# FFN up projection: from two pairs of chunks by Winograd's form to three by Strassen's, spread over three blocks, one sum of weights per pair by accumulating transfers

## The chip, the cores and the metric

The kernel runs on one core of a Trainium2 chip. TensorE (PE) multiplies, VectorE (DVE), ScalarE (ACT) and GpSimd (POOL) do the rest, each engine working through its own instructions in order. Transfers are issued from SyncE's queue (SP), a few from ACT's, and, in the changed kernel, some from POOL's. The metric is the device time of the kernel in microseconds (us); the time before is the median of three runs.

## The reference

Two layers of a decoder trunk. Each layer has an FFN (a), a mixer of three branches, an FFN (b) and a small embedding step. The change is in the FFN alone, which runs four times.

```python
SEQ, D_MODEL, D_FF, DEPTH = 256, 1024, 2816, 2
def swiglu(x, w1, w3, w2):
    return (jax.nn.silu(x @ w1) * (x @ w3)) @ w2
...
h = h + 0.5 * swiglu(rms_norm(h, g_ffn1[i]), w1_a[i], w3_a[i], w2_a[i])
...
h = h + 0.5 * swiglu(rms_norm(h, g_ffn2[i]), w1_b[i], w3_b[i], w2_b[i])
```

## The kernel before

*Numbers.* Every fp32 operand of a matmul is split into a high part (ACT casts it to fp32r: whi, xhi, fhi) and a low part (DVE subtracts: wlo, xlo, flo). mm3 (L102 to L104) makes one product of three matmuls: high by high, high x by low w, low x by high w. In the rows of PE the first name behind the arrow is the weight tile, the second the activations.

*Tiles.* The 2816 columns of an FFN are 11 chunks (c = 0 to 10) of 256 columns of w1 and the same of w3, side by side: 512 columns. The 256 tokens are two blocks (tb). A chunk's weights come as four units of 128x1024 fp32 (512 KB, two rows of k by 512 columns); load() fetches a unit into raw on SP's queue and splits it (L86, L87). A unit is used by 12 matmuls of 128x512, a plain chunk by 48. up(c) runs a whole chunk; up_unit(c, i) runs unit i of it (called unit (c, i) or P(c, i) below), so that other work can stand between the units. gated() makes silu(w1 part) x (w3 part) out of PSUM into pr (L236 on ACT, L238 on DVE). turn(c) (T) transposes a chunk's two pr tiles on PE (L250) into one PSUM bank and splits the result into fhi and flo. down_unit(c, j) (D) fetches a unit of w2 and adds 12 matmuls into the four acc banks. PSUM holds two mm banks, two tr banks and these four. There are 7 slots each for whi and wlo, 4 for raw, 10 for wr (wtile), which holds weights that are summed before they are split, and 4 for t512, which holds products.

*Pairs.* Two neighbouring chunks by two halves of k are a 2x2 block matrix. A fast algorithm makes its product with the 2x2 of tokens by halves of k in 7 products of 12 matmuls each instead of 8. x_forms() makes the sums of x's quarters that it needs: DVE adds high and low parts, rescales the second token block (L297), for which the row scale is spread over the partitions by one matmul with ones (L274) and a copy to rb on ACT, and then forms and splits five quarters (q). winograd(c, fx) fetches the pair's 8 tiles and returns make (the split of a weight form), form (a sum of weights on DVE, L320) and the generator of the products (tr banks; L345 and L352 combine them).

*Order.* Each engine's instructions stand largely in the order in which the program is written; the framework moves some by priority. In an FFN, chunks 0, 1 and 2 come first and plain, x_forms() is called behind chunk 1; then block() runs twice, each time one pair (7, 8 and 9, 10) with eight units of two plain chunks (3, 4 and 5, 6), transposes and down units between them by hand-written tables; at the end come D5, T6, T10, D6, T9, and the last four down units with the update of h.

## Time and profile before

| what | before |
|---|---|
| median of three runs | 1333.03 us (1332.51 to 1333.06) |
| the profiled execution | 1332.86 us |
| its span in the profile | 1331.1 us |
| the fourth FFN | 1112.66 to 1297.00 us |

The span runs from the first to the last instruction in the trace; the execution's own time is 1.8 us longer. In rows of the profile, L12 is line 12 of the kernel, a name left of the arrow is written, names right of it are read, and buffer numbers are left out, so wr stands for every wr tile. A bracket behind a row of the timeline tells how long the engine was idle before it, and what released it.

### The profile page before, as it was taken

What the parts mean: (1) busy time and instruction counts of PE and PEld (TensorE: products, weight loads), DVE (VectorE), ACT (ScalarE), POOL (GpSimd) and SP (SyncE); (2) the same over time, 40 slices, a digit from 0 to 9 for tenths busy, and PEclk for the clock granted to TensorE, in tenths of its full rate; (3) what the DMA queues carried; (4) which work ended last, traced back from release to release, by engine and by line L of the source; (5) the groups of instructions that cost most, each with busy time, mean ns of one, the idle gap of its engine ahead of it and who ended that gap; (6) DMA issues with size and microseconds to landing.
All of it is one profiled execution on the core that took longest, in us unless ns stands there. A gap on an engine that the chain in (4) does not pass through costs nothing.

```text
span 1331.1 us, 17969 instructions
## 1 busy us (share of the span) xinstructions
PE 1312.2 (99%) x6624; PEld 1097.5 (82%) x6624; DVE 994.0 (75%) x1414; ACT 802.8 (60%) x1205; POOL 50.2 (4%) x109
## 2 busy tenths in 40 slices
PE   9999999999999999999999999999999999999997
PEld 7788879978888888887888888898888788888876
DVE  7998755666768789975789986566676677999755
ACT  6665546665775655654756665466667835655645
POOL 1000000001100000000100000000010000000001
PEclk9999999999999999999999999999999999999999
DMA  8774537534455567455566646373444465583542
GB/s 296 274 269 127 187 103 228 171 123 132 147 169 175 161 227 276 122 164 182 163 239 196 217 128 210 103 224 127 159 142 143 144 204 167 206 299 102 180 145 80
DMA packets 67769, 236.63 MB, mean 178 GB/s; under 512 B 8160, under 2 KB 8800, under 8 KB 67680
## 3 DMA queue, kind: packets, MB, share of 16 engines
q1 hardware_dynamic: 67104, 234.39, 54.0%
q8 instruction: 52, 0.85, 0.3%
q10 hardware_dynamic: 576, 1.08, 0.2%
q14 instruction: 37, 0.30, 0.1%
HBM read 234.40 MB, written 1.05 MB: 177 GB/s over the span
## 4 chain that ended last, share of the span: by engine, by line
PE 94%; ACT 2%; DVE 2%; DMA 1%; issue 1%; POOL 0%; SPq 0%; POOLq 0%; ACTq 0%; DVEq 0%
PE mm L102 17%; PE mm L104 17%; PE mm L103 17%; PE acc L102 8%; PE acc L103 8%; PE acc L104 8%; PE tr L104 4%; PE tr L102 4%; PE tr L103 4%; PE tr L250 1%; PE tr L150 1%; ACT whi L86 1%; PE tr L716 1%; DVE wlo L87 1%; DMA h<-in_x 1%
## 5 line engine op out<-in xcount | busy, mean ns | idle before, releaser
L87 DVE TENSOR_TENSOR wlo<-raw,whi 128x1024 fp32r<-128x1024 f32 (+1 forms) x378 | 450.1, 1201 | 137.3 <-ACT whi L86 135.1
L86 ACT CAST whi<-raw 128x1024 fp32r<-128x1024 f32 (+1 forms) x378 | 387.3, 1035 | 198.2 <-PE mm L104 77.5
L102 PE MATMUL mm<-whi,xhi 128*128 128x512 f32 (+1 forms) x760 | 296.0, 393 | 0.0
L103 PE MATMUL mm<-wlo,xhi 128*128 128x512 f32 (+1 forms) x760 | 295.1, 389 | 0.3 <-DVE wlo L87 0.3
L104 PE MATMUL mm<-whi,xlo 128*128 128x512 f32 (+1 forms) x760 | 295.2, 389 | 0.0
L102 PEld LDWEIGHTS mm<-whi,xhi 128*128 128x128 f32 x760 | 143.0, 188 | 30.0 <-DVE sqk L516 0.7
L104 PEld LDWEIGHTS mm<-whi,xlo 128*128 128x128 f32 x760 | 142.8, 188 | 29.7 <-DVE xlo L136 0.7
L103 PEld LDWEIGHTS mm<-wlo,xhi 128*128 128x128 f32 x760 | 142.9, 188 | 28.9 <-DVE wlo L87 0.8
L135 ACT CAST whi<-wr 128x1024 fp32r<-128x1024 f32 (+1 forms) x120 | 121.6, 1023 | 66.9 <-PE acc L104 38.9
L136 DVE TENSOR_TENSOR wlo<-wr,whi 128x1024 fp32r<-128x1024 f32 (+1 forms) x120 | 140.6, 1185 | 24.8 <-ACT whi L135 23.6
L102 PE MATMUL acc<-whi,fhi 128*128 128x512 f32 x352 | 132.0, 393 | 7.7 <-ACT fhi L135 7.7
L103 PE MATMUL acc<-wlo,fhi 128*128 128x512 f32 x352 | 137.9, 392 | 0.4 <-DVE wlo L87 0.4
L104 PE MATMUL acc<-whi,flo 128*128 128x512 f32 x352 | 134.6, 390 | 0.0
L102 PEld LDWEIGHTS acc<-whi,fhi 128*128 128x128 f32 x352 | 65.7, 188 | 23.2 <-ACT fhi L135 9.6
L103 PEld LDWEIGHTS acc<-wlo,fhi 128*128 128x128 f32 x352 | 66.1, 188 | 15.2 <-DVE wlo L87 1.8
L104 PEld LDWEIGHTS acc<-whi,flo 128*128 128x128 f32 x352 | 66.1, 188 | 13.6
L320 DVE TENSOR_TENSOR wr<-wr,wr 128x1024 f32<-128x1024 f32 x64 | 76.3, 1217 | 0.0
L102 PE MATMUL mm<-xhi,whi 128*128 128x256 f32 x256 | 73.8, 288 | 0.0
L104 PE MATMUL mm<-xhi,wlo 128*128 128x256 f32 x256 | 72.5, 283 | 0.0
L103 PE MATMUL mm<-xlo,whi 128*128 128x256 f32 x256 | 72.4, 283 | 0.0
L102 PE MATMUL tr<-whi,q 128*128 128x512 f32 x160 | 63.7, 398 | 0.0
L104 PE MATMUL tr<-whi,q 128*128 128x512 f32 x160 | 62.6, 391 | 0.0
(248 smaller groups left out, 1960.8 us busy)
## 6 DMA issues: line engine op xcount, KB each, us to landing
raw<-in_w13b SPq DMA_DIRECT2D x56, 512.0 KB, 3.7
raw<-in_w13a SPq DMA_DIRECT2D x52, 512.0 KB, 4.2
raw<-in_wg SPq DMA_DIRECT2D x48, 512.0 KB, 3.7
raw<-in_w2a SPq DMA_DIRECT2D x44, 512.0 KB, 4.4
raw<-in_w2b SPq DMA_DIRECT2D x44, 512.0 KB, 4.3
wr<-in_w13a SPq DMA_DIRECT2D x32, 512.0 KB, 6.7
raw<-in_wqk SPq DMA_DIRECT2D x32, 512.0 KB, 4.1
wr<-in_w13b SPq DMA_DIRECT2D x32, 512.0 KB, 6.2
```

Of the source, the lines that this page charges most:

```text
L86: A.copy(hi[:, c], raw[:, c])
L87: V.tensor_tensor(out=lo[:, c], in0=raw[:, c], in1=hi[:, c].bitcast(F32), op=ALU.subtract)
L102: PE.matmul(o, lhs[0], rhs[0], start=first, stop=False, **more)
L103: PE.matmul(o, lhs[0], rhs[1], start=False, stop=False, **more)
L104: PE.matmul(o, lhs[1], rhs[0], start=False, stop=last, **more)
L135: A.copy(hi, t)
L136: V.tensor_tensor(out=lo, in0=t, in1=hi.bitcast(F32), op=ALU.subtract)
L150: PE.transpose(t[:, j * P : (j + 1) * P], h[tb][:, k * P : (k + 1) * P], ident)
L250: PE.transpose(t[:, j * S + tb * P : j * S + (tb + 1) * P], prs[c, tb][:, j * P : (j + 1) * P], ident)
L320: V.tensor_tensor(out=out, in0=a, in1=b, op=ALU.subtract)
L716: PE.transpose(t[:, j * P : (j + 1) * P], e[:, j * P : (j + 1) * P], ident)
```

## The change

Three pairs instead of two, (5, 6), (7, 8) and (9, 10), with Strassen's seven products in the order 1, 2, 5, 3, 6, 7, 4. A pair's quarters are x, y, w, z; the sums of weights are x+=w, then x+=z, w+=z and y+=x, and w+=z is made by two transfers on POOL's queue, which read z again from memory and add it to the tile. Five chunks are left plain: 0 and 1 first, 2, 3 and 4 spread over three blocks. What a block runs is now one list: S is a step of the pair (split the weights of the next product, make a sum, run one product), P a unit of a plain chunk, D a down unit, T a transpose. wr has 12 slots and t512 has 5. The lines behind the FFN are numbered 26 higher.

```diff
--- before.py
+++ after.py
...
         with tc.tile_pool(name=nm("fp"), bufs=3) as fp:
             def wtile():
-                return fp.tile([P, U], F32, tag="wr", name=nm("wr"), bufs=10)
+                return fp.tile([P, U], F32, tag="wr", name=nm("wr"), bufs=12)
             def t512(name):
-                return fp.tile([P, 512], F32, tag="t512", name=nm(name), bufs=4)
+                return fp.tile([P, 512], F32, tag="t512", name=nm(name), bufs=5)
             if first:
                 un0 = start(wtile)
...
                     if tb:
                         V.tensor_tensor(out=v4(t), in0=v4(t), in1=rb[:, None, :].to_broadcast([P, 4, P]), op=ALU.mult)
                 f = {1: [x[:, 0, 0:4, :] for x in (xhi, xlo)], 2: [x[:, 0, 4:8, :] for x in (xhi, xlo)]}
-                V.tensor_tensor(out=s1, in0=a10, in1=a11, op=ALU.add)
+                sub(s1, a10, a11)
                 f[5] = quarter(s1)
                 sub(s1, s1, a00)
                 f[6] = quarter(s1)
                 sub(a10, a00, a10)
                 f[7] = quarter(a10)
-                sub(a01, a01, s1)
+                V.tensor_tensor(out=a01, in0=a01, in1=s1, op=ALU.add)
                 f[3] = quarter(a01)
                 f[4] = quarter(a11)
                 return f
-            def winograd(c, fx):
-                ws, t2s, fw = [], [], {}
-                for u in range(2):
-                    ws.append({(kh, nh): wtile() for kh in range(2) for nh in range(2)})
-                for kh, nh in ((0, 0), (1, 0), (0, 1), (1, 1)):
+            ORDER = (1, 2, 5, 3, 6, 7, 4)
+            def pair(c, bank):
+                t = {q: [wtile() for _ in range(2)] for q in "xywz"}
+                fw = {}
+                quarters = {"x": (0, 0), "y": (1, 0), "w": (0, 1), "z": (1, 1)}
+                def at(q, u):
+                    kh, nh = quarters[q]
+                    return w13[li, c + nh, 2 * kh + u]
+                def fetch(q):
                     for u in range(2):
-                        nc.sync.dma_start(ws[u][kh, nh], w13[li, c + nh, 2 * kh + u])
-                def sub(out, a, b):
-                    V.tensor_tensor(out=out, in0=a, in1=b, op=ALU.subtract)
+                        nc.sync.dma_start(t[q][u], at(q, u))
+                def add(q, other):
+                    for u in range(2):
+                        V.tensor_tensor(out=t[q][u], in0=t[q][u], in1=t[other][u], op=ALU.add)
+                def plus(q, other):
+                    for u in range(2):
+                        nc.gpsimd.dma_start(t[q][u], at(other, u), accum_op=ALU.add)
                 def form(i):
-                    for u, w in enumerate(ws):
-                        if i == 1:
-                            sub(w[0, 0], w[0, 1], w[0, 0])
-                        elif i == 2:
-                            t2s.append(wtile())
-                            sub(t2s[u], w[1, 1], w[0, 0])
-                        elif i == 3:
-                            sub(w[0, 1], w[1, 1], w[0, 1])
-                        else:
-                            sub(w[1, 0], w[1, 0], t2s[u])
+                    if i == 1:
+                        add("x", "w")
+                    elif i == 2:
+                        add("x", "z")
+                    elif i == 3:
+                        plus("w", "z")
+                    else:
+                        add("y", "x")
                 def make(i):
-                    at = {1: (0, 0), 2: (1, 0), 7: (0, 1), 5: (0, 0), 3: (1, 1), 4: (1, 0)}
-                    fw[i] = [split_w(t2s[u] if i == 6 else w[at[i]]) for u, w in enumerate(ws)]
+                    fw[i] = [split_w(w) for w in t[{1: "x", 2: "y", 5: "x", 3: "z", 6: "x", 7: "w", 4: "y"}[i]]]
                 def product(o, i, start=False):
                     for kt in range(4):
                         m = [y[:, (kt % 2) * 512 : (kt % 2) * 512 + 512] for y in fw[i][kt // 2]]
                         mm3(o, [y[:, kt, :] for y in fx[i]], m, start and kt == 0, kt == 3, skip_group_check=True)
-                def add(out, a, b):
-                    V.tensor_tensor(out=out, in0=a, in1=b, op=ALU.add)
+                def sum_(out, a, b, op=ALU.add):
+                    V.tensor_tensor(out=out, in0=a, in1=b, op=op)
                 def products():
-                    o = bank_tr()
+                    o = bank()
                     product(o, 1, True)
                     m1 = t512("m1")
                     A.copy(m1, o)
...
                     product(o, 2)
                     gated(c, 0, o, r[0])
                     yield
-                    o = bank_tr()
+                    o = bank()
+                    product(o, 5, True)
+                    c5 = t512("c5")
+                    A.copy(c5, o)
+                    yield
+                    product(o, 3)
+                    v = t512("v")
+                    A.copy(v, o)
+                    yield
+                    o = bank()
                     product(o, 6, True)
                     u2 = t512("u2")
-                    add(u2, o, m1)
+                    sum_(u2, o, m1)
+                    sum_(v, v, u2, ALU.subtract)
+                    gated(c + 1, 0, v, r[0])
                     yield
                     product(o, 7)
-                    add(m1, o, m1)
+                    sum_(m1, o, m1)
+                    sum_(c5, c5, m1, ALU.subtract)
+                    gated(c + 1, 1, c5, r[0])
                     yield
-                    o = bank_tr()
-                    product(o, 5, True)
-                    c22 = t512("c22")
-                    add(c22, o, m1)
-                    gated(c + 1, 1, c22, r[0])
-                    yield
-                    product(o, 3)
-                    add(u2, o, u2)
-                    gated(c + 1, 0, u2, r[0])
-                    yield
-                    o = bank_tr()
+                    o = bank()
                     product(o, 4, True)
-                    add(m1, o, m1)
+                    sum_(m1, o, m1)
                     gated(c, 1, m1, r[0])
                     yield
-                return make, form, products()
-            def block(wg, plain, turns, downs, then=None):
-                make, form, ps = wg
+                return make, fetch, form, products()
+            def block(now, plan, then=None):
+                make, _, form, ps = now
                 following = None
                 os = []
-                for k in range(8):
-                    if k < 6:
-                        make((2, 6, 7, 5, 3, 4)[k])
-                    if k < 3:
-                        form(k + 2)
-                    if k == 6 and then is not None:
-                        following = winograd(then, fx)
-                    if k == 7 and then is not None:
-                        following[0](1)
-                        following[1](1)
-                    if k < 7:
+                k = 0
+                for kind, *arg in plan:
+                    if kind == "S":
+                        if k < 6:
+                            make(ORDER[k + 1])
+                        if k < 4:
+                            form((1, 2, 3, 4)[k])
+                        if then is not None:
+                            if k == 2:
+                                following = pair(*then)
+                                following[1]("x")
+                            elif k == 3:
+                                following[1]("y")
+                            elif k == 4:
+                                following[1]("w")
+                            elif k == 5:
+                                following[1]("z")
+                            elif k == 6:
+                                following[0](1)
                         next(ps)
-                    if k % 4 == 0:
-                        os = []
-                    up_unit(plain[k // 4], k % 4, os)
-                    if k in downs:
-                        down_unit(*downs[k])
-                    for t in turns.get(k, ()):
-                        turn(t)
+                        k += 1
+                    elif kind == "P":
+                        if arg[1] == 0:
+                            os = []
+                        up_unit(*arg, os)
+                    elif kind == "D":
+                        down_unit(*arg)
+                    else:
+                        turn(*arg)
                 return following
-            for c in range(3):
+            for c in range(2):
                 if first and c == 1:
                     un = []
...
                 if c == 1:
                     acc.extend(bank_acc() for _ in range(4))
                     fx = x_forms()
-                    wg = winograd(7, fx)
+                    wg = pair(5, bank_tr)
+                    for q in "xywz":
+                        wg[1](q)
                 if c >= 1:
                     turn(c - 1)
             wg[0](1)
-            wg[1](1)
-            for j in range(2):
-                down_unit(0, j)
             if first:
                 later()
-            wg = block(
-                wg, (3, 4), {0: [2], 4: [3]},
-                {0: (1, 0), 1: (1, 1), 2: (2, 0), 3: (2, 1), 5: (3, 0), 6: (3, 1)}, 9,
-            )
+            wg = block(wg, [
+                ("S",), ("P", 2, 0), ("D", 0, 0), ("S",), ("P", 2, 1), ("S",), ("D", 0, 1), ("P", 2, 2), ("S",),
+                ("T", 1), ("P", 2, 3), ("S",), ("D", 1, 0), ("S",), ("D", 1, 1), ("S",), ("T", 2),
+            ], (7, bank_tr))
+            wg = block(wg, [
+                ("S",), ("P", 3, 0), ("D", 2, 0), ("S",), ("T", 6), ("P", 3, 1), ("D", 2, 1), ("S",),
+                ("P", 3, 2), ("T", 5), ("D", 6, 0), ("S",), ("P", 3, 3), ("D", 6, 1), ("S",), ("D", 5, 0),
+                ("S",), ("D", 5, 1), ("T", 3), ("S",),
+            ], (9, bank_tr))
             if aside is not None:
                 aside()
-            block(
-                wg, (5, 6), {0: [4], 1: [7], 2: [8], 5: [5]},
-                {1: (4, 0), 2: (4, 1), 3: (7, 0), 4: (7, 1), 5: (8, 0), 6: (8, 1)},
-            )
-            for j in range(2):
-                down_unit(5, j)
-            turn(6)
-            turn(10)
-            for j in range(2):
-                down_unit(6, j)
-            turn(9)
+            wg = block(wg, [
+                ("S",), ("P", 4, 0), ("D", 3, 0), ("S",), ("T", 8), ("P", 4, 1), ("D", 3, 1), ("S",), ("T", 7),
+                ("P", 4, 2), ("D", 8, 0), ("S",), ("P", 4, 3), ("D", 8, 1), ("S",), ("D", 7, 0), ("S",),
+                ("D", 7, 1), ("T", 4), ("S",), ("T", 10),
+            ])
+            block((None, None, None, iter(())), [
+                ("D", 4, 0), ("T", 9), ("D", 4, 1),
+            ])
```

What this moves, at three places of the fourth FFN. First DVE, at the start of block 1. Before:

```order
L87 TENSOR_TENSOR wlo_10835<-raw_10833,whi_10834 128x1024
L136 TENSOR_TENSOR pT_11444<-xg_11445,pT_11443 128x512
L238 SCALAR_TENSOR_TENSOR pr_10719<-mm_10692,r_10503,act_10717 128x256
L87 TENSOR_TENSOR wlo_10841<-raw_10839,whi_10840 128x1024
L238 SCALAR_TENSOR_TENSOR pr_10748<-mm_10721,r_10558,act_10746 128x256
L297 TENSOR_TENSOR wr_10763<-wr_10763,rb_10761 128x512 x2
L136 TENSOR_TENSOR flo_10813<-tr_10814,fhi_10812 128x512
L299 TENSOR_TENSOR wr_10765<-wr_10763 128x512
L284 TENSOR_TENSOR wr_10763<-wr_10764,wr_10763 128x512
```

Before, DVE splits chunk 2's last units (L87, wlo from raw) and gates chunk 1 (L238) ahead of the forms of x, which begin with L297. After, from the forms on (they stand directly behind chunk 1's two rows of L238):

```order
L297 TENSOR_TENSOR wr_10865<-wr_10865,rb_10863 128x512 x2
L136 TENSOR_TENSOR flo_10915<-tr_10916,fhi_10914 128x512
L284 TENSOR_TENSOR wr_10867<-wr_10865 128x512
L284 TENSOR_TENSOR wr_10865<-wr_10866,wr_10865 128x512
L136 TENSOR_TENSOR q_10876<-wr_10867,q_10875 128x512
L284 TENSOR_TENSOR wr_10867<-wr_10867,wr_10866 128x512
L305 TENSOR_TENSOR wr_10866<-wr_10866,wr_10867 128x512
L136 TENSOR_TENSOR q_10881<-wr_10867,q_10880 128x512
L136 TENSOR_TENSOR q_10886<-wr_10865,q_10885 128x512
L136 TENSOR_TENSOR q_10891<-wr_10866,q_10890 128x512
L136 TENSOR_TENSOR q_10895<-wr_10865,q_10894 128x512
L136 TENSOR_TENSOR wlo_10924<-wr_10898,whi_10923 128x1024
```

Eleven rows with twelve operations make the forms (and one flo of chunk 0), and the first weights that DVE splits behind them are the first pair's: wlo from wr, 128x1024.

PE at the same place, before:

```order
L104 MATMUL mm_10721<-whi_10687,xlo 128x512
L274 MATMUL tr_10759<-xg_10757,ones 128x128
L250 MATMUL tr_10814<-ident,pr_10637 128x128 x2
L250 MATMUL tr_10814<-ident,pr_10666 128x128 x2
L102 MATMUL mm_10845<-whi_10822,xhi 128x512
L103 MATMUL mm_10845<-wlo_10823,xhi 128x512
```

and after:

```order
L104 MATMUL mm_10823<-whi_10789,xlo 128x512
L274 MATMUL tr_10861<-xg_10859,ones 128x128
L250 MATMUL tr_10916<-ident,pr_10739 128x128 x2
L250 MATMUL tr_10916<-ident,pr_10768 128x128 x2
L102 MATMUL tr_10941<-whi_10923,xhi 128x512
L103 MATMUL tr_10941<-wlo_10924,xhi 128x512
```

mm and whi from chunk 2 follow the transposes (L250) before, product 1 of the pair (tr and whi from wr) after.

Last, PE's tail. Before:

```order
L104 MATMUL acc_10753<-whi_11945,flo_11838 128x512
L250 MATMUL tr_11964<-ident,pr_11920 128x128 x2
L250 MATMUL tr_11964<-ident,pr_11924 128x128 x2
L250 MATMUL tr_11973<-ident,pr_11799 128x128 x2
L250 MATMUL tr_11973<-ident,pr_11736 128x128 x2
L102 MATMUL acc_10750<-whi_11981,fhi_11962 128x512
L103 MATMUL acc_10750<-wlo_11982,fhi_11962 128x512
```

and after:

```order
L102 MATMUL acc_10852<-whi_12117,fhi_12080 128x512
L103 MATMUL acc_10852<-wlo_12118,fhi_12080 128x512
L250 MATMUL tr_12109<-ident,pr_12016 128x128 x2
L250 MATMUL tr_12109<-ident,pr_12060 128x128 x2
L104 MATMUL acc_10852<-whi_12117,flo_12081 128x512
L102 MATMUL acc_10853<-whi_12117,fhi_12080 128x512
L103 MATMUL acc_10853<-wlo_12118,fhi_12080 128x512
L104 MATMUL acc_10853<-whi_12117,flo_12081 128x512
```

Before, the transposes of chunks 6 and 10 stand side by side, and the next acc matmul reads the fhi that comes of the first of them. After, chunk 10's transposes stand among the matmuls of D(4,0), which read another fhi.

## The prediction

> **What bounds the kernel now.** First the page's busy rows and its chain of waits, then the stalls of TensorE (PE), then one FFN by itself, since the change touches nothing else.

> ```profile
> PE 1312.2 (99%) x6624; PEld 1097.5 (82%) x6624; DVE 994.0 (75%) x1414; ACT 802.8 (60%) x1205; POOL 50.2 (4%) x109
> ...
> PE 94%; ACT 2%; DVE 2%; DMA 1%; issue 1%; POOL 0%; SPq 0%; POOLq 0%; ACTq 0%; DVEq 0%
> ...
> PE acc L102 <- ACT fhi L135: 7.7, 8, 1.2
> ```

> PE is busy 99% of the span and carries 94% of the chain: a matmul taken away is worth its full pitch, and a PE stall costs its full length. The third row (waits of PE: us, times, the longest) is the largest stall inside the FFNs. Now windows over all engines: the fourth FFN, a piece of it with dense VectorE (DVE) work, and a piece of plain matmuls. The columns are length, then busy time of PE, PEld, DVE, ACT and POOL, then the granted clock, the DMA share and GB/s.

> ```profile
> 1112.66:1297.00 184.34, 182.41 (x831) 150.25 (x829) 147.64 (x168) 103.90 (x131) 2.02 (x6) 1.00 0.56 187
> 1142.46:1177.00 34.54, 34.54 (x156) 28.32 (x156) 34.53 (x34) 22.03 (x25) 0.00 (x0) 1.00 0.60 202
> 1192.69:1209.01 16.32, 16.32 (x73) 13.51 (x72) 16.20 (x18) 8.88 (x10) 0.00 (x0) 1.00 0.41 122
> ```

> An FFN takes 184.34 us with PE idle for 1.9 of them. In the third row 72 matmuls of 128x512 take 16.32 us, so the pitch is 0.227 us at a granted clock of 1.00. In the second row DVE is busy 34.53 of 34.54 us and PE loses nothing: DVE can be full without holding PE up.

> **The change part by part.** The sum is made against the profiled execution (span 1331.1, its own time 1332.86 us; the median of the runs is 1333.03, so the forecast carries over within 0.2).

> *Matmuls.* A third pair replaces two plain chunks: 7 products of 12 matmuls, where two plain chunks have 96. That is 12 fewer per FFN, 12 x 0.227 = **-2.72 us**, wholly on PE's path.

> *The tail.* Before, two transposed chunks (L250) stand back to back and the next matmul needs their copies at once:

> ```profile
> 1273.52 1.04 PE L250 MATMUL tr<-ident,pr 128*128 128x128 f32 x8
> 1275.30 0.50 PE L102 MATMUL acc<-whi,fhi 128*128 128x512 f32 x1 [0.74 <-ACT fhi L135]
> ...
> 1280.90 0.60 PE L250 MATMUL tr<-ident,pr 128*128 128x128 f32 x4
> 1282.68 0.50 PE L102 MATMUL acc<-whi,fhi 128*128 128x512 f32 x1 [1.18 <-ACT fhi L135]
> ```

> Transposes cost about 0.09 us each (8 begin and end within 1.04), so from 1273.52 to 1275.30 about 1.08 us pass for nothing, and from 1280.90 to 1282.68 about 1.4; I take 2.3 for both, with the overlap of the last transpose off. The new tail puts chunk 10's transposes among the matmuls of D(4,0) and chunk 9's ahead of D(4,1), which needs neither; 12 matmuls, 2.72 us, cover 1.18. **-2.3 us** per FFN. Nothing else is late there: the weights of the last units are requested early in both.

> *The start of block 1.* This term decides. The forms of x (x_forms) wait for one matmul (L274) behind chunk 1. Their DVE chain, and behind it the split of the first pair's weights, run like this before, in the fourth FFN:

> ```profile
> 1133.42 0.60 PE L250 MATMUL tr<-ident,pr 128*128 128x128 f32 x4
> 1133.77 0.47 PE L102 MATMUL mm<-whi,xhi 128*128 128x512 f32 x1
> ...
> 1134.30 1.29 DVE L297 TENSOR_TENSOR wr<-wr,rb 128x512 f32<-128x512 f32 x2
> 1135.50 0.68 DVE L136 TENSOR_TENSOR flo<-tr,fhi 128x512 fp32r<-128x512 f32 x1
> 1136.11 0.68 DVE L299 TENSOR_TENSOR wr<-wr 128x512 f32<-128x512 f32 x1
> 1136.82 0.69 DVE L284 TENSOR_TENSOR wr<-wr,wr 128x512 f32<-128x512 f32 x1
> 1137.48 0.69 DVE L136 TENSOR_TENSOR q<-wr,q 128x512 fp32r<-128x512 f32 x1
> 1138.20 1.42 DVE L284 TENSOR_TENSOR wr<-wr,wr 128x512 f32<-128x512 f32 x2
> 1139.58 2.50 DVE L136 TENSOR_TENSOR q<-wr,q 128x512 fp32r<-128x512 f32 x4
> 1142.00 0.48 DVE L238 SCALAR_TENSOR_TENSOR pr<-mm,r,act 128x256 f32<-128x256 f32 x1
> 1142.46 2.36 DVE L136 TENSOR_TENSOR wlo<-wr,whi 128x1024 fp32r<-128x1024 f32 x2
> ...
> 1141.02 0.47 ACT L236 ACTIVATE act<-mm,r 128x256 f32<-128x256 f32 x1
> 1141.38 1.99 ACT L135 CAST whi<-wr 128x1024 fp32r<-128x1024 f32 x2
> ```

> Before, PE steps at 1133.77 straight into plain chunk 2 (48 matmuls, 48 x 0.227 = 10.9 us), whose weights were split ahead of the chain; the chain ran beside it and cost nothing. In the new order of instructions chunk 2 is spread over block 1, and behind the transposes of chunk 0 PE has product 1. Its weights are split on DVE and on ScalarE (ACT) behind the whole chain, in all four FFNs. The cover is gone. The chain keeps its 12 operations, since L305 only turns a difference into a sum. ACT no longer has the activation of 1141.02, so its cast of the first tile starts there and ends at 1141.02 + 1.04 = 1142.06; DVE's subtraction follows, 1.22, until 1143.28. PE has one matmul (0.23) to do between, with whi alone. The hole is 1143.28 - 1133.77 - 0.23 = **+9.3 us** per FFN. Bounds: 8.3 us, if the subtraction overlapped the cast wholly, and 10.9, the cover that goes.

> *Behind the hole.* Two things, of which the later counts. On DVE the first split is followed by three more of weights, two sums and then the low half of unit (2,0), at 1.14 us each (2.36 - 1.22): 6.8 us. PE has 26 matmuls until it needs it, 5.9 us: a wait of 0.9. The other is the clock:

> ```profile
> 1323.15 0.28 PE L104 MATMUL mm<-whi,xlo 128*128 128x256 f32 x1
> ...
> 1326.60:1327.00 0.40, 0.00 (x0) 1.00 0.00 0
> 1327.00:1327.40 0.40, 0.00 (x0) 0.56 0.00 0
> ...
> 0.97 4.63 PE L992 MATMUL tr<-ones 128*128 128x128 f32 x20 [0.97 <-POOL mhalf L72]
> 5.47 0.99 PE L102 MATMUL mm<-whi,xhi 128*128 128x512 f32 x2
> 6.30 0.64 PE L103 MATMUL mm<-wlo,xhi 128*128 128x512 f32 x2
> ```

> At the end of the program PE's last matmul ends at 1323.43, and the granted clock falls to half at about 1327.0: 3.6 us of idleness. At its start the matmuls of 5.47 are 0.41 us apart and those from 6.30 on 0.24: some 5.3 us of work pass before PE is at speed. The hole holds 8.3 us without a matmul, so the clock would fall, and 5 us at about half rate lose 2.5. Bounds: 0.9 (the clock doesn't fall: the wait alone) and 2.7. I take **+2.5**, the only rows that show a cold PE; PE is then late enough for the weights.

> [...]

> *Work beside PE.* Per FFN DVE gets 8 more operations of 1024 columns (the splits of six weight tiles, two sums; 8 x 1.14 = 9.1 us) and five more of 512 on products (0.69 each, 3.4 us): about 160 of 185 us, still less dense than the window above. ACT gets six casts (1.0 each) and seven copies: 104 + 11 us. Both hide beside PE; bounds nothing, and one 1.14 us where a split comes last. Between blocks product 1 waits for a PSUM bank that a sum of 0.69 us reads: between 0 and 0.7, I take **+0.3**.

> *Accumulating transfers* (one sum per pair, two of 512 KB on POOL's queue). Before has none. The nearest rows are the plain ones, issue to landing:

> ```profile
> raw<-in_w13b SPq DMA_DIRECT2D x56, 512.0 KB, 3.7
> ...
> wr<-in_w13b SPq DMA_DIRECT2D x32, 512.0 KB, 6.2
> ```

> In block 1 they may start after x+=w, and DVE reaches the split of their result 16 operations later, 15 of about 1.14 and one of 0.48: at least 17.5 us; in blocks 2 and 3 later still. At the price of the plain ones to the same tiles, one behind the other, both have landed after 2 x 6.2 = 12.4; if each took twice that because it reads two operands, after 24.8. I take 12.4, the nearest row, and so **nothing** on the path; bounds 0 and 24.8 - 17.5 = 7.3 per FFN. What they spare DVE is in the list above already.

> *SP's queue.* In the first FFN alone, two weight tiles of chunk 1's down projection now stand behind fetches of the next pair, which wait for tiles to come free. Cost: between 0 and one landing, 3.7; I take 0.5, since only the excess over their lead counts.

> Sum: -2.72 - 2.3 + 9.3 + 2.5 + 0.3 = +7.1 per FFN, x4 = 28.3, and 0.5: 1332.86 + 28.8 = 1361.7, say **1361**.

> **The rivals.** *A, faster: the split runs ahead of the forms.* If the hardware's order let the first pair's weights be split before L274, product 1 would start at 1133.77, and only -2.72 - 2.3 with 0.3 remained: -4.7 x 4, 1314. The point from which it decides: hole and its wake together under 4.7 us per FFN. For it: the tiles are loaded early and nothing in the data ties them to the forms. Against it: engines work their rows in order, and the split's rows stand behind the chain on both; the pair's tiles can't pass it.

> *B, far slower: the accumulating transfers are late.* At 24.8 us each pair, block 1 loses 7.3 and DVE's queue stands still behind the split; blocks 2 and 3, with about 24 us by the same count, lose about 1 each: +9.3 x 4 = 37 on top, about 1399. For it: every transfer now reads its target too. Against it: 17.5 us are nearly three of the slower landings. [...]

> *C, milder: the hole without a colder clock.* Then the wake is 0.9 and all is 1332.86 + 4 x 5.5 + 0.5 = 1355.

> *D, no change:* that the matmuls aren't saved is excluded by the order (48 fewer); for no change the hole and its wake would have to come to about 4.7 us.

> **How the numbers follow.** The forecast 0.62 (1361), C 0.20 (1355), B 0.08 (1399), A 0.07 (1314), D 0.03. The low end is C with the hole at 8.3 instead of 9.3: 1351, and 0.5 less on SP's queue, rounded to 1350. The high end is the forecast with the hole 1.6 longer (10.9, x4 = 6.4), 0.4 more for the bank and 1.14 for a late split, each x4: 1373, and 3.7 for SP: 1377. About 0.15 to 0.2 lies outside. A measurement of this kernel tells about 0.2% from no change: faster 0.07, same 0.03, slower 0.90.

> **What would show it.** In the changed kernel, four PE waits of 8 to 9 us at product 1 of block 1, released by ACT's whi or DVE's wlo; half a clock in a window just behind them; no more wait for fhi in the tail; the FFN otherwise shorter by the 5 us of the first two terms. A wait of DVE or ACT for POOL's queue ahead of product 7 would be rival B. If product 1 starts right behind L250, I am wrong.

## The result and the profile after

| what | before | after |
|---|---|---|
| median of three runs | 1333.03 us | 1355.51 us (1354.1 to 1359.27) |
| the profiled execution, its span | 1332.86, 1331.1 | 1355.51, 1353.7 |
| end of FFN 1, 2, 3, 4 (last update of h) | 195.0, 639.2, 852.7, 1297.0 | 198.7, 649.5, 868.8, 1319.3 |
| what FFN 1, and 2 to 4 with the mixers ahead of them, got longer | | 3.7, 6.6, 5.8, 6.3 |

The ratio is 1.0171 with a 95% interval of 1.0148 to 1.0194: slower, by 22.5 us, where 28 were forecast.

The changed kernel's page, its busy rows and its chain by engine:

```profile
PE 1308.6 (97%) x6576; PEld 1093.2 (81%) x6576; DVE 1042.0 (77%) x1466; ACT 837.2 (62%) x1257; POOL 69.5 (5%) x133
...
PE 91%; DVE 5%; issue 1%; ACT 1%; DMA 1%; SPq 0%; POOLq 0%; POOL 0%; ACTq 0%
```

The 48 matmuls are gone (6576 where there were 6624), but PE's share of the span fell from 99 to 97%, and DVE stands on the chain with 5% instead of 2. PE's largest waits in the changed kernel (us, times, the longest) say for whom:

```profile
PE tr L102 <- ACT whi L135: 32.3, 4, 8.1
PE tr L103 <- DVE wlo L136: 1.9, 4, 0.5
```

Four waits of 8.1 us, one in each FFN, and the tail's waits for fhi (7.7 us before) no longer stand in the list. The place is the one forecast. Here is the fourth FFN of the changed kernel, first PE, then DVE, then ACT, from the timeline:

```profile
1149.39 0.39 PE L274 MATMUL tr<-xg,ones 128*128 128x128 f32 x2
1149.61 0.60 PE L250 MATMUL tr<-ident,pr 128*128 128x128 f32 x4
1158.29 0.80 PE L102 MATMUL tr<-whi,xhi 128*128 128x512 f32 x1 [8.08 <-ACT whi L135]
1159.55 0.80 PE L103 MATMUL tr<-wlo,xhi 128*128 128x512 f32 x1 [0.46 <-DVE wlo L136]
...
1150.50 1.28 DVE L297 TENSOR_TENSOR wr<-wr,rb 128x512 f32<-128x512 f32 x2
...
1155.77 2.50 DVE L136 TENSOR_TENSOR q<-wr,q 128x512 fp32r<-128x512 f32 x4
1158.27 4.63 DVE L136 TENSOR_TENSOR wlo<-wr,whi 128x1024 fp32r<-128x1024 f32 x4
...
1155.12 2.18 ACT L135 CAST q<-wr 128x512 fp32r<-128x512 f32 x4 [1.49 <-DVE wr L284]
1157.20 3.88 ACT L135 CAST whi<-wr 128x1024 fp32r<-128x1024 f32 x4
```

PE is ready at about 1150.0 and steps into product 1 at 1158.29, when ACT has cast the first tile; the second matmul waits once more, for DVE. DVE works without a gap from 1150.50 on, and the split of the first pair's weights is its first row behind the forms: the bracket of PE names ACT's cast, but what PE truly waits for is the chain of forms ahead of it. The granted clock there (length, PE's busy time, clock, DMA share, GB/s; PE alone):

```profile
1150.00:1152.00 2.00, 0.21 (x2) 1.00 0.95 387
1152.00:1153.00 1.00, 0.00 (x0) 0.85 0.09 37
1153.00:1158.00 5.00, 0.00 (x0) 0.50 0.10 18
1158.00:1162.00 4.00, 3.24 (x7) 0.50 0.28 109
1162.00:1163.00 1.00, 1.00 (x4) 0.53 0.00 0
1163.00:1164.00 1.00, 1.00 (x6) 1.00 0.00 0
```

The clock falls to half within the hole, and PE works at half rate from 1158.3 to 1162.9: its matmuls start 0.43 us apart, against 0.23 behind that. Last the accumulating transfers, issue to landing:

```profile
wr<-in_w13a POOLq DMA_DIRECT2D x12, 512.0 KB, 5.6
wr<-in_w13b POOLq DMA_DIRECT2D x12, 512.0 KB, 5.6
```

With a median of 5.6 us they are no slower than the plain ones were (6.2 and 6.7 to the same tiles before). The two of a first block, which are issued 0.9 to 1.1 us apart, land one behind the other, though: the pair is there 9.5 to 11.2 us after the first was issued.

### The profile page after: what moved, and what is told of

It reads as the page before. It is cut to its first block, busy times and chain, and to the rows that moved or that the text cites. A ratio compares the mean times of both kernels' runs of the same rounds, so it can differ in the third digit from the quotient of the medians.

```text
span 1353.7 us, 18041 instructions
## 1 busy us (share of the span) xinstructions
PE 1308.6 (97%) x6576; PEld 1093.2 (81%) x6576; DVE 1042.0 (77%) x1466; ACT 837.2 (62%) x1257; POOL 69.5 (5%) x133
## 3 DMA queue, kind: packets, MB, share of 16 engines
q10 hardware_dynamic: 576, 1.08, 0.2%
## 4 chain that ended last, share of the span: by engine, by line
PE 91%; DVE 5%; issue 1%; ACT 1%; DMA 1%; SPq 0%; POOLq 0%; POOL 0%; ACTq 0%
PE mm L102 15%; PE mm L104 14%; PE mm L103 14%; PE acc L103 8%; PE acc L104 8%; PE acc L102 8%; PE tr L103 6%; PE tr L102 5%; PE tr L104 5%; PE tr L250 1%; PE tr L150 1%; DVE q L136 1%; DVE wlo L136 1%; PE tr L742 1%; DVE wlo L87 1%
## 5 line engine op out<-in xcount | busy, mean ns | idle before, releaser
L87 DVE TENSOR_TENSOR wlo<-raw,whi 128x1024 fp32r<-128x1024 f32 (+1 forms) x346 | 411.4, 1200 | 93.1 <-ACT whi L86 90.8
L86 ACT CAST whi<-raw 128x1024 fp32r<-128x1024 f32 (+1 forms) x346 | 354.3, 1033 | 165.7 <-PE acc L104 52.3
L102 PE MATMUL mm<-whi,xhi 128*128 128x512 f32 (+1 forms) x632 | 247.1, 396 | 0.0
L104 PE MATMUL mm<-whi,xlo 128*128 128x512 f32 (+1 forms) x632 | 245.8, 389 | 0.0
L103 PE MATMUL mm<-wlo,xhi 128*128 128x512 f32 (+1 forms) x632 | 245.6, 389 | 0.0
L135 ACT CAST whi<-wr 128x1024 fp32r<-128x1024 f32 (+1 forms) x176 | 179.9, 1032 | 93.2 <-PE acc L104 53.1
L136 DVE TENSOR_TENSOR wlo<-wr,whi 128x1024 fp32r<-128x1024 f32 (+1 forms) x176 | 207.4, 1198 | 25.7 <-ACT whi L135 24.5
L104 PEld LDWEIGHTS mm<-whi,xlo 128*128 128x128 f32 x632 | 118.7, 188 | 24.8 <-DVE xlo L136 0.7
L102 PEld LDWEIGHTS mm<-whi,xhi 128*128 128x128 f32 x632 | 118.7, 188 | 24.4 <-DVE sqk L542 0.7
L104 PE MATMUL acc<-whi,flo 128*128 128x512 f32 x352 | 137.6, 391 | 0.0
L103 PEld LDWEIGHTS mm<-wlo,xhi 128*128 128x128 f32 x632 | 118.9, 188 | 23.1 <-DVE wlo L136 0.2
L103 PE MATMUL acc<-wlo,fhi 128*128 128x512 f32 x352 | 137.1, 390 | 0.0
L102 PE MATMUL acc<-whi,fhi 128*128 128x512 f32 x352 | 135.2, 392 | 0.0
L102 PE MATMUL tr<-whi,q 128*128 128x512 f32 x240 | 94.1, 392 | 0.0
L104 PE MATMUL tr<-whi,q 128*128 128x512 f32 x240 | 93.6, 390 | 0.0
L103 PE MATMUL tr<-wlo,q 128*128 128x512 f32 x240 | 93.4, 389 | 0.0
L104 PEld LDWEIGHTS acc<-whi,flo 128*128 128x128 f32 x352 | 66.1, 188 | 13.8
L103 PEld LDWEIGHTS acc<-wlo,fhi 128*128 128x128 f32 x352 | 66.1, 188 | 13.5
L102 PEld LDWEIGHTS acc<-whi,fhi 128*128 128x128 f32 x352 | 66.1, 188 | 13.4
L102 PE MATMUL tr<-whi,xhi 128*128 128x512 f32 x96 | 42.3, 440 | 33.0 <-ACT whi L135 32.3
L102 PE MATMUL mm<-xhi,whi 128*128 128x256 f32 x256 | 73.8, 288 | 0.0
## 6 DMA issues: line engine op xcount, KB each, us to landing
wr<-in_w13a SPq DMA_DIRECT2D x48, 512.0 KB, 6.2
raw<-in_wg SPq DMA_DIRECT2D x48, 512.0 KB, 3.8
wr<-in_w13b SPq DMA_DIRECT2D x48, 512.0 KB, 5.8
raw<-in_w2a SPq DMA_DIRECT2D x44, 512.0 KB, 4.4
raw<-in_w2b SPq DMA_DIRECT2D x44, 512.0 KB, 4.3
raw<-in_w13b SPq DMA_DIRECT2D x40, 512.0 KB, 4.3
raw<-in_w13a SPq DMA_DIRECT2D x36, 512.0 KB, 4.6
raw<-in_wqk SPq DMA_DIRECT2D x32, 512.0 KB, 3.8
```

Of the source, the lines that this page charges most:

```text
L86: A.copy(hi[:, c], raw[:, c])
L87: V.tensor_tensor(out=lo[:, c], in0=raw[:, c], in1=hi[:, c].bitcast(F32), op=ALU.subtract)
L102: PE.matmul(o, lhs[0], rhs[0], start=first, stop=False, **more)
L103: PE.matmul(o, lhs[0], rhs[1], start=False, stop=False, **more)
L104: PE.matmul(o, lhs[1], rhs[0], start=False, stop=last, **more)
L135: A.copy(hi, t)
```

## The experiments

Each ratio is to the kernel of before on the same chip, with its 95% interval.

**Forms ahead of chunk 1 in three FFNs.** The changed kernel with

```diff
-                    os0 = up(c, un0 if first and c == 0 else [load(w13[li, c, i]) for i in range(4)], bank_mm)
+                    un = un0 if first and c == 0 else [load(w13[li, c, i]) for i in range(4)]
+                    if c == 1:
+                        fx = x_forms()
+                    os0 = up(c, un, bank_mm)
                 if c == 1:
                     acc.extend(bank_acc() for _ in range(4))
-                    fx = x_forms()
+                    if first:
+                        fx = x_forms()
```

> The changed kernel, with the forms of x called ahead of chunk 1 instead of behind it in the second, third and fourth FFN; the first FFN stays as it was and serves as a control. Theory 1 (the hole is DVE's chain of forms, which stands ahead of the first pair's split and waits for one matmul behind chunk 1): in three FFNs the hole of 8.25 us, the second gap of 1.03 and the slow matmuls behind it (1.96 on the mean) go, 11.2 us each, so 1355.5 - 33.7 = 1322; the first FFN keeps a hole of 8.2 us. Rival (VectorE is too dense, and the chain only moves its cost in front of chunk 1's own splits): new waits of 4 to 8 us in chunk 1, 1335 to 1350.

Measured 1322.98 us, ratio 0.9922 (0.9908 to 0.9937): 33 us off the changed kernel by moving one call. PE's waits in it:

```profile
PE tr L102 <- ACT whi L135: 8.1, 1, 8.1
PE tr L102 <- DVE m L356: 1.0, 2, 0.5
...
PE tr L103 <- DVE wlo L136: 0.5, 1, 0.5
```

Four waits of 8.1 became one, in the first FFN, the control. VectorE does the same work as in the changed kernel, so density was not the matter. A new small wait shows: product 1 of a later block for m, the last sum out of the bank that it takes.

**The same in the first FFN too,** there within chunk 1 (a call behind the sixth of the eight steps of k in its first token block).

```diff
+                        if mid is not None and tb == 0 and kt == 5:
+                            fx.update(mid())
...
-                    up(c, un, bank_acc)
+                    up(c, un, bank_acc, x_forms)
```

> As e1_forms_early, and in the first FFN the forms are called within chunk 1, behind its first token block's sixth step. Theory 1: no hole over 2 us is left, 1355.5 - 44.9 = 1311 to 1313, faster than both kernels. Rival (VectorE too dense): 1325 to 1350.

Measured 1320.31 us, 0.9901 (0.9887 to 0.9916). A miss, of 8 us: the first FFN gained 3.0, not 11, and the stretch from there to the end of the second gave back 1.6. The wait in the first only shrank:

```profile
PE tr L102 <- ACT whi L135: 3.7, 1, 3.7
```

DVE's timeline at this place:

```profile
24.28 0.28 DVE L274 TENSOR_SCALAR xg<-ident,rho 128x128 f32<-128x128 f32 x1
24.47 1.22 DVE L87 TENSOR_TENSOR wlo<-raw,whi 128x1024 fp32r<-128x1024 f32 x1
26.01 1.29 DVE L299 TENSOR_TENSOR wr<-wr,rb 128x512 f32<-128x512 f32 x2 [0.32 <-ACT rb L278]
```

In the first FFN the row scale itself (rho) is ready at 22.8 us only, since DVE waits until 22.7 for the second token block's r from POOL; spread into xg behind a split of weights it is ready at 24.6. The chain, which takes 7.7 us without other work between, starts at 26.0 and can't end before chunk 1 does at 29.4.

**The weights' split ahead of the forms.** The forms still wait for the matmul behind chunk 1; make(1) alone moves.

```diff
-                    fx = x_forms()
+                    fx = {1: [x[:, 0, 0:4, :] for x in (xhi, xlo)], 2: [x[:, 0, 4:8, :] for x in (xhi, xlo)]}
                     wg = pair(5, bank_tr)
                     for q in "xywz":
                         wg[1](q)
+                    wg[0](1)
+                    fx.update(x_forms())
...
-            wg[0](1)
```

> The changed kernel with one move: the split of product 1's weights (make(1)) is called ahead of the forms of x instead of behind them, in all four FFNs; the forms still wait for the matmul behind chunk 1. Theory 1 (the hole is only the place of that split behind the chain on VectorE and ScalarE; the first form is not needed before product 5): no hole at product 1, in the first FFN either: 1355.5 - 44.9 = 1311, up to 1316 with new waits at product 5. Rival (the hole is VectorE's backlog, 7.7 us of chain that must come out somewhere in block 1): the wait moves to product 2 or 5 with 3 to 6 us per FFN, 1325 to 1335.

Measured 1322.1 us, 0.9919 (0.9904 to 0.9934). In FFNs 2, 3 and 4 no wait over 0.3 us is left (439.3, 208.7 and 439.5 us from the end of one to the next, against 444.2, 213.5 and 444.2 before): the chain takes no less time, it only stands where nobody waits for it. In the first FFN the wait came back elsewhere, and that part of the expectation failed; the total lies between the 1316 of the theory and the 1325 of the rival:

```profile
PE mm L102 <- ACT whi L86: 7.8, 1, 7.8
```

There PE stands from 35.2 to 43.0 us for unit (2,0). Its weights landed at 36.8, but ACT casts it behind the last of the forms, at 41.9.

**Chunk 2 plain in front again,** as before, so that block 1 has no units of a plain chunk.

```diff
-            for c in range(2):
+            for c in range(3):
...
-                ("S",), ("P", 2, 0), ("D", 0, 0), ("S",), ("P", 2, 1), ("S",), ("D", 0, 1), ("P", 2, 2), ("S",),
-                ("T", 1), ("P", 2, 3), ("S",), ("D", 1, 0), ("S",), ("D", 1, 1), ("S",), ("T", 2),
+                ("S",), ("D", 0, 0), ("S",), ("S",), ("D", 0, 1), ("S",),
+                ("S",), ("D", 1, 0), ("S",), ("D", 1, 1), ("S",), ("T", 2),
```

> The changed kernel with chunk 2 plain in front again, as before, so that block 1 has no units of a plain chunk. Theory 1 (chunk 2 was the cover of the forms): no hole at product 1, 1355.5 - 44.9 = 1311, if nothing else is late. What may be late is VectorE in block 1: 20 splits and 6 sums of 1.14, 5.4 us of sums of products and gates and a flo of 0.69 are 35.7 us, beside 11 groups of 12 matmuls, 29.9 us; with no lead that costs 5.8 us per FFN, 1334. So between 1311 and 1334, with waits for VectorE inside block 1. Rival (the hole is not a matter of the cover): 1355.

Measured 1324.62 us, 0.9929 (0.9916 to 0.9943), between the two ends. The hole is gone in all four FFNs, and a smaller wait for VectorE has come, as named:

```profile
PE tr L102 <- DVE u L356: 4.7, 4, 1.4
```

So the cover is what the change took away. Spreading chunk 2 over block 1 is worth something too, but less than the hole: FFNs 2 to 4 take 2.1 to 3.4 us longer here than with the weights' split ahead. In each FFN ACT also waits 1.5 to 2.8 us for the second accumulating transfer of block 1, whose lead goes with the units; that PE loses by that isn't shown, since DVE works without a gap up to the sum u that PE waits for.

**TensorE kept at work in the hole.** 30 matmuls, whose result nobody reads, between the transposes and product 1.

```diff
+            o = bank_mm()
+            for i in range(30):
+                PE.matmul(o, xhi[:, 0, i % 8, :], xhi[:, 0, 0:4, :].rearrange("p k t -> p (k t)"), start=i == 0, stop=i == 29)
             wg[0](1)
```

> The changed kernel with 30 more matmuls of 128x512 in each FFN (6.8 us at full rate), into a PSUM bank whose result nobody reads, between the transposes of chunk 0 and product 1: the hole stays, but TensorE works through most of it. Theory (what follows the hole is the clock, 1.96 us per FFN): the matmuls behind the hole run at their pitch of 0.227, 1355.5 - 7.8 = 1348, or 1351 if the wait for the low half of unit (2,0), forecast at 0.9 us, then shows. Rival (the slow matmuls behind the hole come from the weights or the banks): they stay slow, 1355.

Measured 1356.25 us, 1.0178 (1.0161 to 1.0195): no faster than the changed kernel. The trace is of one execution, at 1354.36 us and a mean clock of 0.997; the other three, at 1355.8 to 1359.27, have 0.993 to 0.996. In three of the traced one's four FFNs the clock stayed at 1.00 and the matmuls behind the hole ran at full pitch, as here in the third:

```profile
707.54 0.50 PE L103 MATMUL tr<-wlo,xhi 128*128 128x512 f32 x1 [0.76 <-DVE wlo L136]
707.88 0.40 PE L104 MATMUL tr<-whi,xlo 128*128 128x512 f32 x1
708.12 0.39 PE L102 MATMUL tr<-whi,xhi 128*128 128x512 f32 x1
...
711.01 0.50 PE L102 MATMUL tr<-whi,xhi 128*128 128x512 f32 x1 [0.19 <-ACT m L363]
```

and yet from the first matmul of product 1 to the end of the FFN it took 159.75 us in the first FFN (160.77 in the changed kernel), 160.23 in the second (161.25) and 160.26 in the third (160.43). In the fourth, where the clock fell, it took 162.18 (161.05). The time came back as waits for copies, neither out of the bank of the added matmuls: a tr bank (0.36 us later than its pitch, at 711.01) and fhi (0.89 us, at 751.1). The page's waits have that last one four times, where the changed kernel has none:

```profile
PE acc L102 <- ACT fhi L135: 2.4, 4, 0.7
```

Slow matmuls behind the hole are thus real (2.1, 2.2 and 1.4 us of extra spacing in these three FFNs of the changed kernel), but more than half of their cost stands in for waits that a faster PE would have. Both expectations fell: the clock is the cause of the slow matmuls, and its price in these three FFNs is 0.2 to 1.0 us rather than 2.

**The third sum on VectorE,** no accumulating transfers, in the changed kernel and in the version without holes.

```diff
                     elif i == 3:
-                        plus("w", "z")
+                        add("w", "z")
```

> The changed kernel with w+=z on VectorE as the other sums, no accumulating transfers. Theory 1 (transfers and the sums on VectorE both hide beside TensorE): 1355 within 2 us. Rival (VectorE is the bound in the blocks, and the transfers are what keeps it below): 24 sums of 1.14 us come onto the path, up to 27 us more, 1382. Other rival (the accumulating transfers are late and cost time): 1340 to 1350.

> e7_best with w+=z on VectorE, no accumulating transfers. If the transfers are worth something once the hole is gone: up to 24 x 1.14 = 27 us slower than e7_best, 1345; if VectorE hides the sums, within 3 us of it, 1318 to 1321.

Measured 1357.96 us, 1.0183 (1.0168 to 1.0198), where the changed kernel has 1.0171 (1.0148 to 1.0194); and 1319.96 us, 0.9901 (0.9885 to 0.9918), where its partner below has 0.9892 (0.9877 to 0.9907). Both pairs of intervals overlap: the transfers cost no time that shows, and they are worth no more than some 2 us of 1330.

**The tail alone, in the kernel of before.**

```diff
-            for j in range(2):
-                down_unit(5, j)
+            down_unit(5, 0)
             turn(6)
+            down_unit(5, 1)
             turn(10)
-            for j in range(2):
-                down_unit(6, j)
+            down_unit(6, 0)
             turn(9)
+            down_unit(6, 1)
```

> The kernel of before, with its tail alone in another order: D(5,0), T6, D(5,1), T10, D(6,0), T9, D(6,1) instead of D(5,0), D(5,1), T6, T10, D(6,0), D(6,1), T9. Theory (each group of transposes followed by its own reader costs the copies' time, 2.3 us per FFN): 1333.0 - 9.2 = 1324. Rival (the wait moves to the next reader or to the weights): 1331 to 1333.

Measured 1323.0 us, 0.9918 (0.9904 to 0.9931). The first FFN's tail, PE's timeline:

```profile
172.26 0.60 PE L250 MATMUL tr<-ident,pr 128*128 128x128 f32 x4
172.61 0.48 PE L102 MATMUL acc<-whi,fhi 128*128 128x512 f32 x1
```

PE steps from the transposes into a down unit of another chunk, with no bracket. The profiled span is 9.9 us shorter, 2.5 per FFN. Of the 5.0 us per FFN that matmuls and tail could bring, half needed nothing but this.

**Versions that beat both.** The forms ahead of chunk 1 in three FFNs, and chunk 2 in front in the first alone:

```diff
-            for c in range(2):
+            for c in range(3 if first else 2):
...
+                ("S",), ("D", 0, 0), ("S",), ("S",), ("D", 0, 1), ("S",),
+                ("S",), ("D", 1, 0), ("S",), ("D", 1, 1), ("S",), ("T", 2),
+            ] if first else [
```

> e1_forms_early (forms ahead of chunk 1 in three FFNs) with chunk 2 plain in front in the first FFN, as in e6_cover. The first FFN ended at 193.3 us in e6_cover and at 198.3 in e1_forms_early: 1323.0 - 5.0 = 1318. Rival (the later FFNs take the gain back): 1321 to 1323.

Measured 1318.79 us, 0.9892 (0.9877 to 0.9907), as added up. Then with units (3,0) and (4,0) ahead of product 1 of their blocks:

```diff
-                ("S",), ("P", 3, 0), ("D", 2, 0), ("S",),
+                ("P", 3, 0), ("S",), ("D", 2, 0), ("S",),
...
-                ("S",), ("P", 4, 0), ("D", 3, 0), ("S",),
+                ("P", 4, 0), ("S",), ("D", 3, 0), ("S",),
```

> e7_best with units (3,0) and (4,0) ahead of product 1 in the second and third block. Theory: product 1 waits there for the PSUM bank that the last sum of the block before it reads (0.68 us at 522.6 and 1171.1 in e1_forms_early); the unit covers that: 1.4 to 2.7 us less than e7_best, 1315 to 1317. Rival: the unit's own split then comes too late, no gain or slower.

Measured 1316.71 us, 0.9877 (0.9862 to 0.9892): the wait for m is gone from PE's list, and the expected 2 us with it, though the intervals of the two overlap. FFNs 2, 3 and 4 end 438.9, 208.3 and 438.8 us after the one before, which is 5.3, 5.2 and 5.4 less than before the change. Last, that with the first FFN as in the version ahead of it (the unit is moved where first is false alone):

> e9_unit_first, with the unit ahead of product 1 in the second, third and fourth FFN alone; the first FFN is that of e7_best, which ended at 192.9 us against 194.2 in e9_unit_first. Theory: the terms add, 1316.7 - 1.3 = 1315.4. Rival (the first FFN's end varies by as much from build to build): 1316 to 1317.

Measured 1316.84 us, 0.9882 (0.9865 to 0.9898): no difference from the one before, the rival.

## Why the prediction was right, and where it was off

*The matmuls and the tail* (-2.72 and -2.3 per FFN): right. Without the hole, with nothing but one call moved, FFNs 2 to 4 are 4.4 to 4.9 us shorter than before, where the two terms and the 0.3 for the bank make 4.7; where the bank's wait is covered as well, they are 5.2 to 5.4 shorter, and the two terms make 5.0. The tail alone measured 2.5.

*The hole* (+9.3): right in place, cause and size. PE's spacing gives 8.25 us to the first matmul of product 1 and 1.03 to the second, 9.28. That the chain stands ahead of the split is shown twice over, by moving the chain and by moving the split; that chunk 2 was the cover, by putting it back.

*Behind the hole* (+2.5): the slow matmuls were there, with 2.1, 2.2, 1.4 and 1.7 us of extra spacing in the four FFNs, so the term was somewhat large. The mistake was in what the clock is worth: the prediction set 2.5 with the clock down against 0.9 without, 1.6 apart, and the run with the clock kept up shows 0.2 to 1.0, since other waits took most of the gain. Rival C's 1355 agrees with the measured 1355.5 by accident; its condition, a clock that stays up, was not met. The two delays that the prediction read from before, 3.6 us of idleness to half the clock and 5.3 us of work to the full, both lie within what the four holes show: 2.5 to 5.3 us of idleness passed before the clock fell, and 4.0 to 5.7 us from the first matmul behind the hole to the rise.

*The work beside PE and the transfers* (nothing): right for the transfers, 9.5 to 11.2 us for a pair in block 1 (forecast 12.4) against 17.5 of lead, and shown by replacing them. The 0.3 for the bank was there too: three waits of 0.2, some 0.4 each by the spacing, and up to 1.3 at one place where no hole makes PE late.

*The first FFN* (the same +7.1, and 0.5 for SP's queue): this is the term that was mis-sized. It measured +3.7, 3.9 of the 6 us by which the forecast was too long. Its hole is as long as the others (8.25), and no wait for the two weight tiles behind SP's fetches came; but the prediction charged the hole and left out what the old plan lost in block 1 of that FFN alone. These waits of before:

```profile
PE acc L103 <- DVE wlo L87: 0.9, 2, 0.5
...
PE tr L102 <- ACT m L352: 0.6, 1, 0.6
...
PE mm L103 <- DVE wlo L87: 0.3, 1, 0.3
```

are 1.8 us in the list. The 0.5 of them at 23.9 us stands in both kernels; the others, at 46.2, 47.1 and 55.6, went: 1.3 us in the list, 2.1 by the spacing of PE's matmuls. With SP's 0.5 and the bank's 0.3, which never came in this FFN, and a wake of 2.1 instead of 2.5 that makes some 3.3 of the 3.9; the rest is not traced. The other three FFNs came to +18.7 us where 21.3 were forecast: the wake and the bank together about 2.2 each instead of 2.8, and the tail saved 0.2 more.

*The rivals.* A, that the split runs ahead of the forms, didn't happen by itself. The run that makes it happen, with the weights' split ahead, bears out its price in FFNs 2 to 4 (4.9, 4.8 and 4.7 us shorter than before, forecast 4.7), and the first FFN, which with its wait of 7.8 for unit (2,0) got 2.5 longer, is what keeps it from 1314. B, late transfers, is excluded: no wait of PE, DVE or ACT for POOL's queue stands ahead of product 7, and in the changed kernel the pairs of block 1 land in 9.5 to 11.2 us beside a DVE that is busy 97 to 100% of these stretches.

## What to carry to other kernels

When work is spread "evenly", ask what the block that is broken up had been covering: here 10.9 us of plain matmuls covered a 7.7 us chain of forms that stood in no list of waits, and the cover was worth more than the 12 matmuls saved. The cure was a matter of one call's place, in front of the cover or behind the split: here the split of the weights stood behind the chain on DVE and ACT and waited with it, though it needed nothing from it (with its call moved ahead, PE's wait of 8.1 us at product 1 was gone). And a stall's wake should be priced by what waits next, not by the slow work that is seen in it.

## What the runs showed of the hardware

The clock did not fall after a fixed idleness. In the changed kernel PE's last matmul before the four holes ended at 29.9, 480.2, 700.3 and 1150.2, and the clock fell at about 33.1, 483.7, 705.5 and 1152.7: 3.3, 3.5, 5.3 and 2.5 us later. The third, by windows of PE:

```profile
704.00:705.00 1.00, 0.00 (x0) 1.00 0.00 0
705.00:706.00 1.00, 0.00 (x0) 0.77 0.00 0
```

In the run with the filled hole PE idled only 1.2 to 1.3 and 0.8 us with one matmul between in FFNs 2 to 4, and 1.9 and 0.8 in the first; in three FFNs the clock stayed, in the fourth it fell:

```profile
1156.00:1158.00 2.00, 1.24 (x3) 0.74 0.32 123
1158.00:1160.00 2.00, 2.00 (x7) 0.50 0.00 0
```

So gaps of 1.2 to 1.3 and 0.8 us went with a fall of the clock in one FFN of this run, and with none in two others.
